# Per-row variance of a 64 MB tensor: how 88 of 128 columns are summed and squared, and by which engine

## The chip, the core and the metric

The kernel runs on one core of one Trainium2 chip. The core has engines with their own instruction queues that meet only through semaphores: VectorE (DVE), ScalarE (ACT), GpSimd (POOL) and SyncE (SP), which here only starts transfers. TensorE isn't used. Data comes from the chip's main memory (HBM) into an on-chip memory of 128 partitions (SBUF) over 16 DMA engines. PSUM is a second, smaller on-chip memory that ACT and DVE can write.

The metric is the time of the program on the device in microseconds (us). The kernel before takes 165.54 us, the median of 3 runs (165.43 to 165.58).

## The reference

```python
x: (32, 512, 1024) float32
mean_sq = np.mean(x**2, axis=-1)
sq_mean = np.mean(x, axis=-1)**2
return (mean_sq - sq_mean).astype(np.float32)
```

So each of 16384 rows of 1024 numbers is reduced to one number, its variance. 67.1 MB are read and 64 KB are written, and every number read is used once.

## The kernel before

**Tiling.** The 16384 rows are spread over 128 partitions, 128 rows to each. A "column" is one row of each partition: 128 x 1024 numbers, 0.52 MB. Column numbers run from 0 to 127. In memory the first 16 columns form one block and the other 112 a second one (`BLOCKS`), so that inside a block the columns of one partition lie next to each other. `load` (L40) brings n neighbouring columns in one transfer from SP's queue: n x 4 KB in a row for each partition.

**Body.** Columns 0 to 103 come in 13 loads of 8 columns (L143 to L151), into three rotating tiles `xt`. A load into a tile waits until DVE and ACT are through with what the tile held before. Of each 8 columns, ACT takes 3 or 2 (in turn) and DVE the other 5 or 6.

- An ACT column (`act_cols`, L117) takes two instructions over 1024 numbers. A Copy (L121) whose accumulator gives minus the mean, and then a Square (L129) which takes that mean as its bias operand and whose accumulator gives the variance, written straight into the result tile `mv`. The elementwise results go to scrap tiles: the Copies of a group to `junk[0]`, `junk[1]`, `junk[2]`, all Squares to `junk[3]`. Reading the accumulator is an instruction of its own in the profile (ACTIVATION_READ_ACCUMULATOR).
- A DVE column takes two bn_stats (BATCH_NORM_STATS2, L111), one for each half of 512 numbers. Each gives counts, means and sums of squared deviations.
- For the body's DVE columns POOL joins these statistics into variances (`join`, L81 to L108), ten small instructions for many columns at once.

**End.** The last 24 columns have a tile of their own, `xt_end`, and come in loads of 6, 6, 4, 3, 2 and 1 columns (`END_LOADS`), which `END_WHO` deals out to ACT (A) and DVE (D). The statistics of the first two of these loads are joined by POOL. After those, DVE joins each column's two halves itself with a bn_aggr (BATCH_NORM_AGGREGATE, L169). The last two columns come in halves, each half a transfer, so that DVE can begin on the first half (L173 to L179).

**Stores.** Columns 0 to 15 are stored from ACT's queue, the others from SP's queue when all is done (L52).

**What sets the order.** Each engine's queue is in order. The instructions are put into the queues by a planner that follows the order of the program and may move an instruction forward where it expects its engine to be idle; it also adds the semaphore waits. The store from ACT, last in the program, stands in ACT's queue at 140.9 us, before ACT's work on `xt_end`. SP's loads too wait now and then for an earlier transfer, on account of a limited number of transfers in flight.

Of the kernel before, what the change touches and what calls it, by code (L numbers as in the profile page):

```python
# [10 lines left out]
@with_exitstack  # L11
def kernel(
    ctx: ExitStack,
    tc: tile.TileContext,
    x: bass.AP,
    out: bass.AP,
):

    nc = tc.nc
    P = nc.NUM_PARTITIONS
    FP32 = mybir.dt.float32
    ACTF = mybir.ActivationFunctionType
    ALU = mybir.AluOpType

    xf = x.flatten_outer_dims()
    N, D = xf.shape
    assert N % P == 0
    ncols = N // P  # L30
    H = D // 2


    SMALL = 16
    BLOCKS = [(0, SMALL, 0), (SMALL, ncols - SMALL, SMALL * P)]

    def block_of(c):
        return next(b for b in BLOCKS if b[0] <= c < b[0] + b[1])

    def load(dst, c0, n, f0=0, f=D):  # L40

        b0, pitch, row0 = block_of(c0)
        assert c0 + n <= b0 + pitch
        ap = [[pitch * D, P], [D, n], [1, f]] if n > 1 else [[pitch * D, P], [1, f]]
        nc.sync.dma_start(  # L45
            out=dst,
            in_=dataclasses.replace(xf, offset=(row0 + c0 - b0) * D + f0, ap=ap),
        )

    def store(engine, block):  # L50
        b0, pitch, row0 = block
        engine.dma_start(  # L52
            out=dataclasses.replace(out, offset=row0, ap=[[pitch, P], [1, pitch]]),
            in_=mv[:, 1, b0 : b0 + pitch],
        )

    GROUP = 8
    NGROUPS = 13
    END0 = GROUP * NGROUPS
    ACT_OF_GROUP = (3, 2)  # L60

    END_LOADS = [6, 6, 4, 3, 2, 1]
    END_WHO = "AADDDDAADDDDDADDDADADA"
    BATCH = (2, 6, 2)

    xpool = ctx.enter_context(tc.tile_pool(name="xpool", bufs=3))
    spool = ctx.enter_context(tc.tile_pool(name="spool", bufs=4))
    opool = ctx.enter_context(tc.tile_pool(name="opool", bufs=1))

    mv = opool.tile([P, 2, ncols], FP32)  # L70
    neg_mean = opool.tile([P, ncols], FP32)
    junk = [opool.tile([P, D], mybir.dt.bfloat16, name=f"junk{i}") for i in range(4)]
    xt_end = opool.tile([P, ncols - END0, D], FP32)
    stats_of = {}

    def stats_block(name, groups, each):

        st = opool.tile([P, groups * each, 2, 6], FP32, name=name)
        return st

    def join(st, groups, each, first, step, skip):  # L81

        n = groups * each
        part = st.rearrange("p n h (e s) -> p n (h e) s", s=3)
        mean, m2 = part[:, :, :, 1], part[:, :, :, 2]
        two = opool.tile([P, n, 2], FP32, name=f"two{first}")
        mu = opool.tile([P, n, 1], FP32, name=f"mu{first}")
        dev = opool.tile([P, n, 4], FP32, name=f"dev{first}")
        g = nc.gpsimd
        g.tensor_tensor(out=two, in0=mean[:, :, 0:2], in1=mean[:, :, 2:4], op=ALU.add)  # L90
        g.tensor_tensor(out=mu, in0=two[:, :, 0:1], in1=two[:, :, 1:2], op=ALU.add)
        g.tensor_scalar(out=mu, in0=mu, scalar1=0.25, scalar2=None, op0=ALU.mult)  # L92
        g.tensor_tensor(out=dev, in0=mean, in1=mu.to_broadcast([P, n, 4]), op=ALU.subtract)  # L93
        g.tensor_tensor(out=dev, in0=dev, in1=dev, op=ALU.mult)  # L94
        g.tensor_scalar(out=dev, in0=dev, scalar1=D / 4.0, scalar2=None, op0=ALU.mult)  # L95
        g.tensor_tensor(out=dev, in0=dev, in1=m2, op=ALU.add)  # L96
        g.tensor_tensor(out=two, in0=dev[:, :, 0:2], in1=dev[:, :, 2:4], op=ALU.add)  # L97
        g.tensor_tensor(out=mu, in0=two[:, :, 0:1], in1=two[:, :, 1:2], op=ALU.add)
        var = mv[:, 1, first : first + groups * step].rearrange(
            "p (g k) -> p g k", k=step  # L100
        )[:, :, skip : skip + each]
        g.tensor_scalar(  # L102
            out=var,
            in0=mu.rearrange("p (g k) o -> p g (k o)", k=each),
            scalar1=1.0 / D,
            scalar2=None,
            op0=ALU.mult,
        )  # L108

    def dve_half(stats, h, xh):  # L110
        nc.vector.bn_stats(out=stats[:, h, :], in_=xh)  # L111

    def dve_halves(stats, xcol):
        dve_half(stats, 0, xcol[:, :H])
        dve_half(stats, 1, xcol[:, H:])

    def act_cols(cols):  # L117

        s = D ** -0.5
        for i, (xcol, c) in enumerate(cols):  # L120
            nc.scalar.activation(  # L121
                out=junk[i],
                in_=xcol,
                func=ACTF.Copy,
                scale=-s / D,
                accum_out=neg_mean[:, c : c + 1],
            )
        for i, (xcol, c) in enumerate(cols):
            nc.scalar.activation(  # L129
                out=junk[3],  # L130
                in_=xcol,
                func=ACTF.Square,
                scale=s,
                bias=neg_mean[:, c : c + 1],
                accum_out=mv[:, 1, c : c + 1],
            )

    body = []
    for par in range(2):
        groups = len(range(par, NGROUPS, 2))  # L140
        each = GROUP - ACT_OF_GROUP[par]
        body.append((stats_block(f"stats{par}", groups, each), groups, each))
    for g in range(NGROUPS):  # L143
        c0 = g * GROUP
        xt = xpool.tile([P, GROUP, D], FP32, name="xt")
        load(xt, c0, GROUP)
        skip = ACT_OF_GROUP[g % 2]
        act_cols([(xt[:, k, :], c0 + k) for k in range(skip)])
        st, _, each = body[g % 2]
        for k in range(skip, GROUP):  # L150
            dve_halves(st[:, g // 2 * each + k - skip, :, :], xt[:, k, :])  # L151
    for par, (st, groups, each) in enumerate(body):
        join(st, groups, each, par * GROUP, 2 * GROUP, ACT_OF_GROUP[par])

    nb, step, skip = BATCH
    each = step - skip
    st_end = stats_block("stats_end", nb, each)
    k = 0
    for b, n in enumerate(END_LOADS):
        load(xt_end[:, k : k + n, :] if n > 1 else xt_end[:, k, :], END0 + k, n)  # L160
        mine = range(k, k + n)
        act_cols([(xt_end[:, j, :], END0 + j) for j in mine if END_WHO[j] == "A"])
        for j in mine:
            if END_WHO[j] == "D" and b < nb:
                dve_halves(st_end[:, b * each + j - k - skip, :, :], xt_end[:, j, :])
            elif END_WHO[j] == "D":
                stats = spool.tile([P, 2, 6], FP32, name="stats")
                dve_halves(stats, xt_end[:, j, :])
                nc.vector.bn_aggr(out=mv[:, :, END0 + j], in_=stats)  # L169
        if b == nb - 1:  # L170
            join(st_end, nb, each, END0, step, skip)
        k += n
    for j in range(k, ncols - END0):  # L173
        stats = spool.tile([P, 2, 6], FP32, name="stats")
        for h in range(2):
            xh = xt_end[:, j, h * H : (h + 1) * H]
            load(xh, END0 + j, 1, h * H, H)
            dve_half(stats, h, xh)
        nc.vector.bn_aggr(out=mv[:, :, END0 + j], in_=stats)  # L179

    store(nc.scalar, BLOCKS[0])
    store(nc.sync, BLOCKS[1])
# [30 lines left out]
```

## Time and profile before

| | us |
|---|---|
| median of 3 runs | 165.54 |
| span of the profiled execution, first to last instruction | 163.5 |
| DVE, ACT, POOL busy in it | 106.1, 94.9, 10.2 |
| first load of 8 columns in, engines start | 12.74 |
| last aggregate of DVE ends | 160.84 |
| final store issued | 160.98 |

The profile shows one execution. The run's time is some 2 us longer than its span, since it includes what lies before the first and after the last instruction; the profiled execution has no separate time beside its span. In the lists, a line of the timeline gives the start, the duration and the instruction, with its output and inputs, and in brackets how long the engine was idle before and what ended that. Instructions of one engine may overlap a little at their ends, so what one more of them costs is the distance from start to start, which is shorter than the duration. "128x512" is 128 partitions by 512 numbers.

### The profile page before, as it was taken

What the parts mean: (1) busy time and instruction counts of PE and PEld (TensorE: products, weight loads), DVE (VectorE), ACT (ScalarE), POOL (GpSimd) and SP (SyncE); (2) the same over time, 40 slices, a digit from 0 to 9 for tenths busy, and PEclk for the clock granted to TensorE, in tenths of its full rate; (3) what the DMA queues carried; (4) which work ended last, traced back from release to release, by engine and by line L of the source; (5) the groups of instructions that cost most, each with busy time, mean ns of one, the idle gap of its engine ahead of it and who ended that gap; (6) DMA issues with size and microseconds to landing.
All of it is one profiled execution on the core that took longest, in us unless ns stands there. A gap on an engine that the chain in (4) does not pass through costs nothing.

```text
span 163.5 us, 462 instructions
## 1 busy us (share of the span) xinstructions
DVE 106.1 (65%) x182; ACT 94.9 (58%) x165; POOL 10.2 (6%) x34
## 2 busy tenths in 40 slices
DVE  0008559393793917949097682949559396859993
ACT  3008756195733937349390693809755195499892
POOL 0000000000000000000000000000000635302200
DMA  7899898998999999999999999999999999999970
GB/s 257 385 481 417 385 513 385 417 481 385 481 417 385 485 409 393 497 393 425 465 393 473 417 393 505 393 401 489 393 465 425 421 391 475 391 440 409 408 291 14
DMA packets 3602, 67.19 MB, mean 411 GB/s; under 512 B 656, under 2 KB 656, under 8 KB 1296
## 3 DMA queue, kind: packets, MB, share of 16 engines
q1 hardware_dynamic: 3456, 67.17, 96.3%
q10 hardware_dynamic: 144, 0.01, 0.1%
q14 instruction: 2, 0.02, 0.0%
HBM read 67.11 MB, written 0.07 MB: 411 GB/s over the span
## 4 chain that ended last, share of the span: by engine, by line
DMA 79%; DVE 11%; ACT 8%; issue 0%; SPq 0%
DMA xt<-in_x_dram 62%; DMA xt_end<-in_x_dram 17%; DVE stats L111 10%; ACT junk L129 4%; ACT junk L121 4%; DVE mv L179 0%; SPq L45 0%
## 5 line engine op out<-in xcount | busy, mean ns | idle before, releaser
L111 DVE BATCH_NORM_STATS2 stats<-xt 128x6 f32<-128x512 f32 x142 | 85.5, 678 | 50.7 <-DMA xt<-in_x_dram 50.7
L121 ACT ACTIVATE junk<-xt 128x1024 bf16<-128x1024 f32 x33 | 34.5, 1046 | 59.2 <-DMA xt<-in_x_dram 59.2
L129 ACT ACTIVATE junk<-xt,neg_mean 128x1024 bf16<-128x1024 f32 x33 | 37.7, 1142 | 0.6
L111 DVE BATCH_NORM_STATS2 stats_end<-xt_end 128x6 f32<-128x512 f32 x16 | 9.7, 680 | 3.7 <-DMA xt_end<-in_x_dram 3.7
L121 ACT ACTIVATE junk<-xt_end 128x1024 bf16<-128x1024 f32 x8 | 8.4, 1046 | 5.0 <-POOL mv L102 4.2
L111 DVE BATCH_NORM_STATS2 stats<-xt_end 128x6 f32<-128x512 f32 x16 | 10.1, 666 | 0.1
L129 ACT ACTIVATE junk<-xt_end,neg_mean 128x1024 bf16<-128x1024 f32 x8 | 9.2, 1144 | 0.2
L90 POOL TENSOR_TENSOR two<-stats 128x72 f32<-128x72 f32 (+1 forms) x2 | 0.8, 406 | 131.3 <-DVE stats L111 131.3
L129 ACT ACTIVATION_READ_ACCUMULATOR junk<-xt,neg_mean 128x1 f32 x33 | 6.2, 186 | 0.0
L121 ACT ACTIVATION_READ_ACCUMULATOR junk<-xt 128x1 f32 x33 | 6.2, 186 | 0.0
L121 ACT ACT_TABLE_LOAD x1 | 1.3, 1283 | 0.7 <-PEq L197 0.7
L121 ACT ACTIVATION_READ_ACCUMULATOR junk<-xt_end 128x1 f32 x8 | 1.5, 186 | 0.0
L129 ACT ACTIVATION_READ_ACCUMULATOR junk<-xt_end,neg_mean 128x1 f32 x8 | 1.5, 186 | 0.0
L95 POOL TENSOR_SCALAR dev<-dev 128x144 f32<-128x144 f32 (+2 forms) x3 | 1.4, 472 | 0.3
L169 DVE BATCH_NORM_AGGREGATE mv<-stats 128x2 f32<-128x12 f32 x6 | 1.2, 203 | 0.1
L94 POOL TENSOR_TENSOR dev<-dev 128x144 f32<-128x144 f32 (+2 forms) x3 | 1.1, 362 | 0.2
L96 POOL TENSOR_TENSOR dev<-dev,stats 128x144 f32<-128x144 f32 (+1 forms) x2 | 1.1, 528 | 0.2
L93 POOL TENSOR_TENSOR dev<-stats,mu 128x144 f32<-128x144 f32 (+1 forms) x2 | 0.9, 470 | 0.2
L102 POOL TENSOR_SCALAR mv<-mu 128x36 f32<-128x36 f32 (+2 forms) x3 | 0.9, 287 | 0.3
L92 POOL TENSOR_SCALAR mu<-mu 128x36 f32<-128x36 f32 (+2 forms) x3 | 0.9, 284 | 0.3
L97 POOL TENSOR_TENSOR two<-dev 128x72 f32<-128x72 f32 (+2 forms) x3 | 0.8, 276 | 0.2
L90 POOL TENSOR_TENSOR two<-stats_end 128x16 f32<-128x16 f32 x1 | 0.2, 233 | 8.9 <-DVE stats_end L111 8.9
(9 smaller groups left out, 2.7 us busy)
## 6 DMA issues: line engine op xcount, KB each, us to landing
xt<-in_x_dram SPq DMA_DIRECT2D x13, 4096.0 KB, 22.2
xt_end<-in_x_dram SPq DMA_DIRECT2D x2, 3072.0 KB, 32.2
xt_end<-in_x_dram SPq DMA_DIRECT2D x1, 2048.0 KB, 40.0
xt_end<-in_x_dram SPq DMA_DIRECT2D x1, 1536.0 KB, 43.2
xt_end<-in_x_dram SPq DMA_DIRECT2D x1, 1024.0 KB, 45.1
xt_end<-in_x_dram SPq DMA_DIRECT2D x4, 256.0 KB, 15.3
xt_end<-in_x_dram SPq DMA_DIRECT2D x1, 512.0 KB, 36.7
out_dram<-mv SPq DMA_DIRECT2D x1, 56.0 KB, 1.6
```

Of the source, the lines that this page charges most:

```text
L90: g.tensor_tensor(out=two, in0=mean[:, :, 0:2], in1=mean[:, :, 2:4], op=ALU.add)
L92: g.tensor_scalar(out=mu, in0=mu, scalar1=0.25, scalar2=None, op0=ALU.mult)
L93: g.tensor_tensor(out=dev, in0=mean, in1=mu.to_broadcast([P, n, 4]), op=ALU.subtract)
L94: g.tensor_tensor(out=dev, in0=dev, in1=dev, op=ALU.mult)
L95: g.tensor_scalar(out=dev, in0=dev, scalar1=D / 4.0, scalar2=None, op0=ALU.mult)
L96: g.tensor_tensor(out=dev, in0=dev, in1=m2, op=ALU.add)
L97: g.tensor_tensor(out=two, in0=dev[:, :, 0:2], in1=dev[:, :, 2:4], op=ALU.add)
L102: g.tensor_scalar(out=var, in0=mu.rearrange("p (g k) o -> p g (k o)", k=each), scalar1=1.0 / D, scalar2=None, op0=ALU.mult,)
L111: nc.vector.bn_stats(out=stats[:, h, :], in_=xh)
L121: nc.scalar.activation(out=junk[i], in_=xcol, func=ACTF.Copy, scale=-s / D, accum_out=neg_mean[:, c : c + 1],)
L129: nc.scalar.activation(out=junk[3], in_=xcol, func=ACTF.Square, scale=s, bias=neg_mean[:, c : c + 1], accum_out=mv[:, 1, c : c + 1],)
L169: nc.vector.bn_aggr(out=mv[:, :, END0 + j], in_=stats)
```

## The change

The work is dealt out anew, in three batches, by a letter for each column.

- S (97 columns): DVE only sums the column. One `tensor_reduce` does it for all S columns of a load, so for 16 x 1024 numbers per partition in the first four loads. ACT squares the column and gets the mean of the squares from its accumulator.
- A (10 columns): ACT squares the column, and also gets the sum by a Copy.
- J (12 columns): two bn_stats, joined by POOL.
- D (8 columns): two bn_stats and a bn_aggr on DVE.

For S and A columns POOL computes mean square minus squared mean (`moments`) for a whole batch: a product, a scaling, and one subtraction for each load of the batch that has such columns (7, 4 and 4). ACT's scrap output is four rotating tiles in PSUM in float32, 8 KB less SBUF than the bf16 ones before; its Square has no bias operand any more. The loads are 16 columns four times, then 8 three times, then 8, 8, 6, 5, then 4, 3, 3, 2; the 5 columns 110 to 114 straddle two tiles and are two transfers. All data goes into three rotating tiles of 16 columns. The last column comes in pieces of 512, 256, 128 and 128 numbers, with a bn_stats each and one bn_aggr.

```diff
-    GROUP = 8
-    NGROUPS = 13
-    ACT_OF_GROUP = (3, 2)
-    END_LOADS = [6, 6, 4, 3, 2, 1]
-    END_WHO = "AADDDDAADDDDDADDDADADA"
+    BATCHES = [
+        ["S" * 16] * 4 + ["S" * 8] * 3,
+        ["SSSAAJJJ", "SSSAAJJJ", "SSAJJJ", "SAJJJ"],
+        ["ADDD", "ADD", "ADD", "AD"],
+    ]
+    LAST = [512, 256, 128, 128]
+    SLOT = 16
...
-    junk = [opool.tile([P, D], mybir.dt.bfloat16, name=f"junk{i}") for i in range(4)]
-    xt_end = opool.tile([P, ncols - END0, D], FP32)
+    ppool = ctx.enter_context(tc.tile_pool(name="ppool", bufs=1, space=bass.MemoryType.PSUM))
+    junk = [ppool.tile([P, D], FP32, name=f"junk{i}") for i in range(4)]
+    def act(xcol, func, scale, accum):
+        nonlocal njunk
+        nc.scalar.activation(
+            out=junk[njunk % len(junk)], in_=xcol, func=func, scale=scale, accum_out=accum
+        )
+        njunk += 1
+
+    def moments(b, total, meansq, runs):
+        g = nc.gpsimd
+        n = total.shape[1]
+        sq = opool.tile([P, n], FP32, name=f"sq{b}")
+        g.tensor_tensor(out=sq, in0=total, in1=total, op=ALU.mult)
+        g.tensor_scalar(out=sq, in0=sq, scalar1=1.0 / (D * D), scalar2=None, op0=ALU.mult)
+        at = 0
+        for c0, m in runs:
+            g.tensor_tensor(
+                out=mv[:, 1, c0 : c0 + m],
+                in0=meansq[:, at : at + m],
+                in1=sq[:, at : at + m],
+                op=ALU.subtract,
+            )
+            at += m
...
+    def stats_of(st, xcol):
+        for h in range(2):
+            nc.vector.bn_stats(out=st[:, h, :], in_=xcol[:, h * H : (h + 1) * H])
+
+    def slot(c):
+        i = c // SLOT
+        if i not in tiles:
+            tiles[i] = xpool.tile([P, SLOT, D], FP32, name="xt")
+        return tiles[i], c % SLOT
...
+        for who in loads:
...
+            if ns:
+                xt, k = slot(c)
+                nc.vector.tensor_reduce(
+                    out=total[:, im : im + ns],
+                    in_=xt[:, k : k + ns, :],
+                    axis=AXIS.X,
+                    op=ALU.add,
+                )
...
+            for j, w in enumerate(who):
+                if w in "SA":
+                    act(cols[j], ACTF.Square, D**-0.5, meansq[:, im : im + 1])
+                    if w == "A":
+                        act(cols[j], ACTF.Copy, 1.0, total[:, im : im + 1])
+                    im += 1
+                elif w == "J":
+                    stats_of(st[:, ij, :, :], cols[j])
+                    ij += 1
+                else:
+                    st1 = opool.tile([P, 2, 6], FP32, name=f"one{c + j}")
+                    stats_of(st1, cols[j])
+                    nc.vector.bn_aggr(out=mv[:, :, c + j], in_=st1)
+            c += n
+        if nm:
+            moments(b, total, meansq, mruns)
+        if nj:
+            join(b, st, jruns)
...
+    for h, f in enumerate(LAST):
+        load(xt[:, k, f0 : f0 + f], c, 1, f0, f)
+        nc.vector.bn_stats(out=st1[:, h, :], in_=xt[:, k, f0 : f0 + f])
+        f0 += f
+    nc.vector.bn_aggr(out=mv[:, :, c], in_=st1)
```

`join` keeps its nine steps before the last and now ends with one scaling for each load of its batch (4).

## The prediction

> **What bounds the kernel now.** I read the page first: busy shares, slices, chain, loads.
>
> ```profile
> DVE 106.1 (65%) x182; ACT 94.9 (58%) x165; POOL 10.2 (6%) x34
> DMA  7899898998999999999999999999999999999970
> DMA 79%; DVE 11%; ACT 8%; issue 0%; SPq 0%
> xt<-in_x_dram SPq DMA_DIRECT2D x13, 4096.0 KB, 22.2
> ```
>
> No engine is full; the transfers are, from slice 2 to slice 38. So the kernel is the load stream plus what follows its end. The stretches by window agree (columns: length, DVE, ACT, POOL busy, clock, DMA share, GB/s):
>
> ```profile
> 22.40:120.40 98.00, 66.24 (x110) 57.01 (x100) 0.00 (x0) 1.00 1.01 433
> 157.00:158.00 1.00, 0.92 (x3) 0.97 (x2) 0.00 (x0) 1.00 1.05 385
> 159.00:160.00 1.00, 0.97 (x4) 0.97 (x3) 0.00 (x0) 1.00 0.02 6
> ```
>
> Then the timeline, for landing times, prices and the tail (start, length, instruction):
>
> ```profile
> 12.74 1.06 ACT L121 ACTIVATE junk<-xt 128x1024 bf16<-128x1024 f32 x1 [10.74 <-DMA xt<-in_x_dram]
> 13.80 1.04 ACT L121 ACTIVATE junk<-xt 128x1024 bf16<-128x1024 f32 x1
> 14.75 0.18 ACT L121 ACTIVATION_READ_ACCUMULATOR junk<-xt 128x1 f32 x1
> 17.13 1.15 ACT L129 ACTIVATE junk<-xt,neg_mean 128x1024 bf16<-128x1024 f32 x1
> 18.41 1.15 ACT L129 ACTIVATE junk<-xt,neg_mean 128x1024 bf16<-128x1024 f32 x1
> ...
> 130.18 1.06 ACT L121 ACTIVATE junk<-xt 128x1024 bf16<-128x1024 f32 x1 [5.12 <-DMA xt<-in_x_dram]
> ...
> 150.03 0.20 POOL L91 TENSOR_TENSOR mu<-two 128x8 f32<-128x8 f32 x1
> 150.32 0.24 POOL L92 TENSOR_SCALAR mu<-mu 128x8 f32<-128x8 f32 x1
> 150.64 0.25 POOL L93 TENSOR_TENSOR dev<-stats_end,mu 128x32 f32<-128x32 f32 x1
> ...
> 151.60 1.24 DVE L111 BATCH_NORM_STATS2 stats<-xt_end 128x6 f32<-128x512 f32 x2
> 152.75 0.20 DVE L169 BATCH_NORM_AGGREGATE mv<-stats 128x2 f32<-128x12 f32 x1
> 152.86 0.64 DVE L111 BATCH_NORM_STATS2 stats<-xt_end 128x6 f32<-128x512 f32 x1
> ...
> 160.63 0.21 DVE L179 BATCH_NORM_AGGREGATE mv<-stats 128x2 f32<-128x12 f32 x1
> 160.98 0.35 SPq L52 DMA_DIRECT2D out_dram<-mv  x1
> ```
>
> What to see. Column 8 is in at 12.74, column 104 at 130.18: 1.2233 us a column, so n columns are in at 12.74 + 1.2233(n - 8); n = 125 gives 155.87, and ACT did stop waiting for that load at 155.86. A Copy takes 1.04 start to start; two end 2.19 after their load (14.93 - 12.74). Squares stand 1.28 apart because all write junk 3. Two bn_stats halves and an aggregate take 1.26 (151.60 to 152.86), a half 0.60. Small POOL steps that follow from each other take 0.29 and 0.32. The final store issues 0.14 after the last aggregate (160.84).
>
> The sum goes against this execution, span 163.5; the median of the runs is 165.54, 2.04 more, which I carry over unchanged.
>
> **The load stream.** 20 loads instead of 23, the same bytes. SP's three issues fewer (0.33 to 0.43 each) lie beside a busy queue: nothing. In the body a load waits for the slot three earlier: the fourth 16 columns need slot 0, free at about 39.6, while the queue holds work until 61.7. Three slots cover it; were a slot held until the queue ran dry, each late microsecond would be lost. SP's waits on earlier transfers (12.1 us once, on the small store from ACT) stay: the last loads then issued at 149.9 and 150.3, and landed in time. Whether rows of 64 KB move at another rate than rows of 32 KB no row shows. Ends: 455 GB/s, the best stretch of ten (92 to 102), or 385, the stretch with the shortest rows. I take the same rate, since share 1.01 leaves no gap between transfers to remove.
>
> **The first loads.** DVE and ACT begin at 22.53 (n = 16) instead of 12.74. 9.8 us of free engine time are given away, and the question is whether each catches up before the tail.
>
> **ACT.** Removed: 41 Copies and 41 biased Squares. Added: 107 Squares (97 S, 10 A) and 10 Copies. A Square without a bias tile, into four rotating outputs in PSUM, has no row, and no row writes PSUM: lower end 0.95 (Copy less its accumulator's 0.09), upper 1.28 (Squares as they stand). I take the Copy's 1.04, because the reasons for 1.28 (one shared output, an operand from a tile) are both taken away. Sixteen cost 16.6 against 19.6 of landing. Slot 3 lands at 81.2: done 97.9; the three loads of 8 at 106.2, 114.5, 122.8; the next 7 instructions at 130.1, when n = 104 lands (130.2). Caught up; the excess is hidden. The store that ACT issues waits for POOL's first result, two or three microseconds about 124, which the later loads absorb (7.3 of work per 9.8).
>
> The Trainium skill, ScalarE: Activation LUTs, under "What ACT_TABLE_LOAD costs", gives 186 ns + 0.833 N for immediate scale and bias and some 93 ns more for a pointer operand: 1.04 and 1.13 at N = 1024, and the durations here, 1040 and 1147, agree within 15 ns. Were the zero bias still a pointer, two Squares at the end would by that be late by about 0.1.
>
> **DVE.** Removed: 174 half-column bn_stats and 8 aggregates. Added: sums over 97 columns (11 instructions), 24 halves for J, 16 halves and 8 aggregates for D, four pieces and one aggregate for the last column. A sum over 16 x 1024 has no row; the nearest is bn_stats. Upper end: 0.60 for 512 as it stands, 1.204 a column. Lower: less 0.11, the start-to-start share of an aggregate (152.75 to 152.86), 0.98 a column. I take 0.07 as the fixed part (0.678 long, 0.60 apart): 1.06 a column, 17.0 per slot. Slot 3 is then done at 98.2, the loads of 8 at 106.7, 115.2, 123.7, then 6.8 each to 130.5 and 137.3; n = 110 lands at 137.5. Caught up, with little to spare.
>
> The Trainium skill, VectorE: DVE Perf Modes, "Rules for kernel authors", speaks against the part: expect 1x from tensor_reduce, the slowest DVE operation. At that page's 0.96 GHz a slot would be 17.07 us, still under 19.6; by it the sum is the same. No run here shows it yet.
>
> **POOL ahead of the tail.** Removed: three joins of 10 steps. Added: 9 steps for columns 0 to 87, 6 and 13 for columns 88 to 114. The last of these start when DVE has its last J (148.1): 13 x 0.33 = 4.3, done at 152.4, eight microseconds before POOL is wanted again. Nothing, unless DVE is late.
>
> **The tail, on the path.** Columns 125 and 126 come in one load, in at 12.74 + 119 x 1.2233 = 158.31. ACT then does Square and Copy of column 125: 2.19, so 160.50. Now POOL is on the path, which it wasn't: the last A columns get their variance from it. The wake-up is 0.08 (149.63 to 149.71). Product 0.29, scaling 0.32, then four subtractions of one column each. They don't depend on each other, and no row shows such a run: upper end 0.29 apart as dependent steps (sum 1.68), lower the 0.03 between the constants' memsets at the start (sum 0.90). I take 0.20, their own length: 0.29 + 0.32 + 3 x 0.20 + 0.20 = 1.41. POOL ends at 160.50 + 0.08 + 1.41 = 161.99, and the store goes at 162.13.
>
> DVE beside it: two D columns from 155.89 to 158.41, column 126 to 159.67, then 0.60 + 0.33 + 0.20 + 0.27 for the pieces (slope as above) and 0.21 for the aggregate: 161.3. The pieces have landed by then: the first half-column of before came at 157.81 where the rate says 157.70, so four pieces at 0.11 extra each are in at 160.0, before DVE reads the last at 160.8. The cut of the last column is worth nothing: DVE still arrives through column 126.
>
> **Sum.** Store at 162.13 instead of 160.98: +1.15. Forecast 165.54 + 1.15 = 166.7. Its own range: POOL's ends -0.5 and +0.3 (DVE's 161.3 holds from below at +0.5), ACT's -0.2 and +0.2: 166.0 to 167.2.
>
> **Rivals.**
> Faster: longer rows speed up the loads. Place: the first 64 columns, 78.3 us. It decides once they run 1.9% faster (1.5 us); at 455 instead of 433 GB/s it's 3.8 us less, 162.9; half that 164.8. For it: stretches of 441 and 455. Against: share 1.01, and 32 KB and 24 KB rows both at 1.22 us a column.
> DVE falls behind: from slot 3 to the end of column 124 there are 49 r + 14.4 (J) + 8.8 (seven D) in 77.2, so it decides from r = 1.10 a column. At 1.204 the end moves by 5.1 past 161.3: store 166.5, total 171.1. For it: the thin margin. Against: a fixed part of nothing in bn_stats isn't credible.
> ACT falls behind: from about 1.18 a column; at 1.28 it goes without a break from 22.5, 117 x 1.28 = 149.8, to 172.3, some 177.4 in all. For it: the Squares of now. Against: their shared output is gone.
> No change: POOL's steps overlap, sum 0.9, and the loads gain 0.3 to 0.7: 165.6 to 166.0.
>
> **Chances.** Forecast 0.58; DVE behind 0.12; ACT behind 0.05; either behind by less, 167.2 to 168.5, 0.04; no change 0.07; loads faster 0.14. Faster or slower means by over 0.2% (0.33 us), about what can be told from no change: faster 0.14, same 0.07, slower 0.79. The range 165.0 to 169.5 leaves out most of the faster case and the worse half of the engines behind.
>
> **What would show it.** Right: DMA share near 1 until 158; the sum of 16 columns near 17 us; Squares 1.04 apart; ACT and DVE waiting for loads again after 137; POOL last before the store, its subtractions after 160.5. Wrong: DVE or ACT without idle time from 81 to the end; the load of column 126 in at 157 or sooner; POOL done before DVE.

## The result, and the profile after

The changed kernel takes 166.38 us (median of 4 runs, 166.18 to 166.54) against 165.56 us before: 1.0049 times as long, with a 95% interval of 1.0035 to 1.0064. It's slower by 0.82 us; the forecast was 1.15 us slower, 166.7. A second comparison of the same two kernels, made later, gave 1.0055 (1.0041 to 1.0069).

The page's view of busy shares, transfers and chain after the change:

```profile
DVE 130.9 (80%) x64; ACT 123.8 (75%) x235; POOL 7.5 (5%) x38
...
DMA  7989996996998899699699998999989999999950
...
DMA 58%; DVE 37%; ACT 1%; POOL 1%; issue 0%; POOLq 0%; ACTq 0%; SPq 0%
...
xt<-in_x_dram SPq DMA_DIRECT2D x5, 4096.0 KB, 31.3
```

DVE and ACT are much busier, yet the transfers go on to slice 38 as before. Four slices of the first half show only 6 tenths, but over longer stretches little is missing: the share is 0.97 from 20 to 60 us (1.00 before) and 1.00 from 60 to 100, and the first 64 columns are in by 80.79, no later than before (81.61). The 37% that the chain gives to DVE is not a loss by itself: a chain that is followed backwards passes through sums that had no waiting between them, while the loads ran beside them. SP's wait for the small store from ACT's queue, now 17.6 us instead of 12.1, isn't one either: the share is 1.00 from 130 to 156, and the load of columns 125 and 126 comes on time. POOL, which wasn't in the chain before, is in it now with 1%. The end of the timeline shows why (start, length, instruction):

```profile
158.37 1.03 ACT L73 ACTIVATE junk<-xt 128x1024 f32<-128x1024 f32 x1 [0.31 <-DMA xt<-in_x_dram]
...
159.42 1.01 ACT L73 ACTIVATE junk<-xt 128x1024 f32<-128x1024 f32 x1
159.67 0.68 DVE L196 BATCH_NORM_STATS2 stlast<-xt 128x6 f32<-128x512 f32 x1
160.26 0.20 DVE L183 BATCH_NORM_AGGREGATE mv<-one 128x2 f32<-128x12 f32 x1
160.37 0.76 DVE L196 BATCH_NORM_STATS2 stlast<-xt 128x6 f32<-128x256 f32 x3
160.37 0.18 ACT L73 ACTIVATION_READ_ACCUMULATOR junk<-xt 128x1 f32 x1
160.64 0.20 POOL L83 TENSOR_TENSOR sq<-total 128x4 f32<-128x4 f32 x1 [7.92 <-ACT junk L73]
160.93 0.23 POOL L84 TENSOR_SCALAR sq<-sq 128x4 f32<-128x4 f32 x1
161.16 0.27 DVE L198 BATCH_NORM_AGGREGATE mv<-stlast 128x2 f32<-128x24 f32 x1
161.24 0.62 POOL L87 TENSOR_TENSOR mv<-meansq,sq 128x1 f32<-128x1 f32 x4
161.88 0.35 SPq L58 DMA_DIRECT2D out_dram<-mv  x1
```

Columns 125 and 126 are there at 158.3, where the rate of the kernel before has them too. ACT needs until 160.55 for column 125, POOL until 161.86, and only then does the store go, at 161.88 instead of 160.98. DVE is through at 161.43, so it lies 0.4 under POOL.

What the engines waited for (total, times, longest), and DVE's timeline in the middle:

```profile
...
ACT junk L73 <- DMA xt<-in_x_dram: 33.0, 8, 20.7
...
DVE total L161 <- DMA xt<-in_x_dram: 29.1, 4, 22.7
ACT junk L73 <- POOL mv L87: 3.0, 1, 3.0
DVE one L127 <- DMA xt<-in_x_dram: 1.2, 2, 0.7
```

```profile
61.45 17.22 DVE L161 TENSOR_REDUCE total<-xt 128x16 f32<-128x16384 f32 x1 [2.23 <-DMA xt<-in_x_dram]
80.79 46.26 DVE L161 TENSOR_REDUCE total<-xt 128x16 f32<-128x16384 f32 x5 [2.13 <-DMA xt<-in_x_dram]
...
148.43 1.88 DVE L127 BATCH_NORM_STATS2 one<-xt 128x6 f32<-128x512 f32 x3 [0.52 <-DMA xt<-in_x_dram]
...
155.81 1.88 DVE L127 BATCH_NORM_STATS2 one<-xt 128x6 f32<-128x512 f32 x3 [0.69 <-DMA xt<-in_x_dram]
```

A sum of 16 columns takes 17.2. From 80.79 on DVE has no pause until the one of 0.52 before 148.43: it did catch up with the loads, but only just.

This profiled execution is the quickest of the four; its span is 164.4, and its time is 166.18, 1.78 more than the span. The median span is 164.6. For the kernel before, the median span beside the later runs is 163.5 and the part outside it 2.0 (1.95 to 2.00 in three sets). So the span grew by 1.1 us, and 0.2 came back outside it.

### The profile page after: what moved, and what is told of

Read it like the earlier page. It is cut to its first block, busy times and chain, and to the rows that moved or that the text cites. A ratio compares the mean times of both kernels' runs of the same rounds, so it can differ in the third digit from the quotient of the medians.

```text
span 164.4 us, 426 instructions
## 1 busy us (share of the span) xinstructions
DVE 130.9 (80%) x64; ACT 123.8 (75%) x235; POOL 7.5 (5%) x38
## 4 chain that ended last, share of the span: by engine, by line
DMA 58%; DVE 37%; ACT 1%; POOL 1%; issue 0%; POOLq 0%; ACTq 0%; SPq 0%
DMA xt<-in_x_dram 51%; DVE total L161 37%; DMA out_dram<-mv 8%; ACT junk L73 1%; POOL sq L84 0%; POOL mv L87 0%; POOL sq L83 0%; POOLq L227 0%; ACTq L227 0%; SPq L51 0%; ACTq L73 0%; POOLq L87 0%
## 5 line engine op out<-in xcount | busy, mean ns | idle before, releaser
L73 ACT ACTIVATE junk<-xt 128x1024 f32<-128x1024 f32 x117 | 117.8, 1007 | 36.0 <-DMA xt<-in_x_dram 33.0
L161 DVE TENSOR_REDUCE total<-xt 128x16 f32<-128x16384 f32 (+4 forms) x11 | 104.7, 9551 | 29.1 <-DMA xt<-in_x_dram 29.1
L73 ACT ACTIVATION_READ_ACCUMULATOR junk<-xt 128x1 f32 x117 | 21.9, 187 | 0.0
L127 DVE BATCH_NORM_STATS2 st<-xt 128x6 f32<-128x512 f32 x24 | 14.6, 677 | 0.0
L127 DVE BATCH_NORM_STATS2 one<-xt 128x6 f32<-128x512 f32 x16 | 10.0, 664 | 1.2 <-DMA xt<-in_x_dram 1.2
L87 POOL TENSOR_TENSOR mv<-meansq,sq 128x16 f32<-128x16 f32 (+5 forms) x15 | 2.5, 206 | 0.2
L183 DVE BATCH_NORM_AGGREGATE mv<-one 128x2 f32<-128x12 f32 x8 | 1.6, 199 | 0.1
L196 DVE BATCH_NORM_STATS2 stlast<-xt 128x6 f32<-128x128 f32 (+2 forms) x4 | 1.4, 402 | 0.0
L84 POOL TENSOR_SCALAR sq<-sq 128x88 f32<-128x88 f32 (+2 forms) x3 | 0.9, 316 | 0.3
L115 POOL TENSOR_SCALAR mv<-mu 128x3 f32<-128x3 f32 x4 | 0.8, 232 | 0.1
```

What stands on the lines that cost most here:

```text
L73: nc.scalar.activation(out=junk[njunk % len(junk)], in_=xcol, func=func, scale=scale, accum_out=accum)
L84: g.tensor_scalar(out=sq, in0=sq, scalar1=1.0 / (D * D), scalar2=None, op0=ALU.mult)
L87: g.tensor_tensor(out=mv[:, 1, c0 : c0 + m], in0=meansq[:, at : at + m], in1=sq[:, at : at + m], op=ALU.subtract,)
L115: g.tensor_scalar(out=mv[:, 1, c0 : c0 + m], in0=mu[:, at : at + m, 0], scalar1=1.0 / D, scalar2=None, op0=ALU.mult,)
L127: nc.vector.bn_stats(out=st[:, h, :], in_=xcol[:, h * H : (h + 1) * H])
L161: nc.vector.tensor_reduce(out=total[:, im : im + ns], in_=xt[:, k : k + ns, :], axis=AXIS.X, op=ALU.add,)
```

## The experiments

Theory: the whole loss lies after the last whole load, and its cause is that POOL's six steps for the last A columns now stand between ACT and the store. DVE's end, 0.4 under it, comes next. Rivals: the new loads and the late start of the engines cost time in the body; or the loads set the end whatever is done.

**POOL taken out of the end** (`t_direct`). The last batch's A columns become B columns: ACT makes the variance itself.

```diff
-        ["ADDD", "ADD", "ADD", "AD"],
+        ["BDDD", "BDD", "BDD", "BD"],
...
+                elif w == "B":
+                    nm1 = opool.tile([P, 1], FP32, name=f"nm{c + j}")
+                    act(cols[j], ACTF.Copy, -(D**-0.5) / D, nm1)
+                    nc.scalar.activation(
+                        out=junk[njunk % len(junk)], in_=cols[j], func=ACTF.Square,
+                        scale=D**-0.5, bias=nm1, accum_out=mv[:, 1, c + j : c + j + 1],
+                    )
```

> The changed kernel, but the four A columns of the last batch (115, 119, 122, 125) get their variance from ACT alone, by a Copy and a Square with the mean as bias, so POOL has nothing after the join of columns 88 to 114. Theory (POOL's last six steps are what the store waits for, and DVE's end at 161.43 lies just under them): the store issues at 161.45 instead of 161.88, the time is about 0.4 us less than the changed kernel's, 166.0. Rival (the new load stream or the body is what costs): the store stays at 161.9 and the time at 166.4.

Measured: 165.97 us, 0.4 less than the changed kernel; 1.0030 times the kernel before (1.0018 to 1.0041). The timeline's end:

```profile
158.60 1.03 ACT L73 ACTIVATE junk<-xt 128x1024 f32<-128x1024 f32 x1 [0.23 <-DMA xt<-in_x_dram]
...
160.84 0.19 ACT L180 ACTIVATION_READ_ACCUMULATOR junk<-xt,nm 128x1 f32 x1
161.30 0.27 DVE L206 BATCH_NORM_AGGREGATE mv<-stlast 128x2 f32<-128x24 f32 x1
161.71 0.35 SPq L58 DMA_DIRECT2D out_dram<-mv  x1
```

The time is as expected. The loads of this execution came 0.2 later than in the first profile, so the store at 161.71 belongs beside the 162.11 of the changed kernel's second profile below, where ACT starts on column 125 at the same 158.60: 0.4 sooner. DVE now ends last, at 161.57, and the store follows 0.14 later, where it followed POOL by 0.02. So of the 1.1 us by which the span grew, POOL's steps account for 0.4. The rest stays, because DVE, which has column 126 and the last column to do, ended only 0.4 before POOL.

**POOL made longer** (`t_pool_long`).

```diff
+        for _ in range(4 if b == 2 else 0):
+            g.tensor_scalar(out=sq, in0=sq, scalar1=1.0, scalar2=None, op0=ALU.mult)
```

> The changed kernel with four more POOL steps in the last batch (the scaled squares are multiplied by 1.0 four times). Theory: every one of them, 0.31 us from start to start, is on the path: store at 161.88 + 1.25 = 163.1, time 167.6. Rival (DVE, ACT or the loads set the end): POOL has time to spare and the time stays at 166.4.

Measured: 167.65 us, 1.27 more than the changed kernel (1.23 more than its second measurement); 1.0132 (1.0119 to 1.0146). Four steps of 0.31 make 1.24, so each is on the path:

```profile
161.32 0.27 DVE L200 BATCH_NORM_AGGREGATE mv<-stlast 128x2 f32<-128x24 f32 x1
161.48 1.14 POOL L86 TENSOR_SCALAR sq<-sq 128x4 f32<-128x4 f32 x4
162.70 0.61 POOL L89 TENSOR_TENSOR mv<-meansq,sq 128x1 f32<-128x1 f32 x4
163.34 0.35 SPq L58 DMA_DIRECT2D out_dram<-mv  x1
```

**The end of the kernel before on the new body** (`t_old_end`).

```diff
-        ["ADDD", "ADD", "ADD", "AD"],
+        ["D", "BDDD", "BDD", "BD", "B"],
-    LAST = [512, 256, 128, 128]
+    LASTS = [[512, 512], [512, 512]]
```

> The changed kernel up to column 114, and from there the end of the kernel before: loads of 1, 4, 3, 2, 1 columns with D and biased ACT columns, and the last two columns in halves. Theory (all of the loss lies after the last whole load): store at 161.0 to 161.1, time 165.5 to 165.7, the same as the kernel before. Rival (starting the engines 9.9 us later, or loads of 16 columns, costs): still 0.4 us or more above the kernel before.

Measured: 165.33 us; 0.9987 times the kernel before (0.9979 to 0.9996).

```profile
157.92 1.38 DVE L205 BATCH_NORM_STATS2 stlast<-xt 128x6 f32<-128x512 f32 x2
...
160.72 0.21 DVE L207 BATCH_NORM_AGGREGATE mv<-stlast 128x2 f32<-128x12 f32 x1
161.07 0.35 SPq L58 DMA_DIRECT2D out_dram<-mv  x1
```

The store is back at 161.07. So columns 0 to 114 in the new form cost nothing, though both engines start ten microseconds later: the loss was all in the end. The 0.2 us below the expectation isn't in the span (median 163.6, against 163.5 before) but outside it (1.78 against 2.00).

**The cut of the last column** (`t_direct_512`), on the version without POOL in the end.

```diff
-    LAST = [512, 256, 128, 128]
+    LAST = [512, 512]
```

> As the run with the direct A columns, and the last column in two halves instead of 512, 256, 128, 128. Theory (DVE reaches the last column late, through column 126, so the small pieces only add instructions): DVE ends 0.1 to 0.2 us sooner, store at 161.3, time 165.8. Rival (the cut of the last column saves waiting for data): later than with four pieces, by 0.2 to 0.4 us.

Measured: 166.00 us, 1.0030 (1.0020 to 1.0041), the same as with four pieces; 165.8 was expected. From the last whole column's bn_stats to the end DVE took 2.74 (158.73 to 161.47) against 2.92 (158.65 to 161.57) with four pieces: 0.18 sooner, as the theory has it, but the loads of this execution were 0.08 later, and the medians don't show the rest. What is shown is that the small pieces gain nothing.

**Shorter first loads** (`b_loads8`).

```diff
-        ["S" * 16] * 4 + ["S" * 8] * 3,
+        ["S" * 8] * 11,
```

> The changed kernel with the first 64 columns in eight loads of 8 columns instead of four of 16, each with its own sum of 8 columns (two loads share a slot). Theory (the stream moves at one rate whatever the length of a row, and a start at 12.8 instead of 22.7 is hidden, since both engines catch up before the end anyway): store within 0.2 us of 161.9, time 166.2 to 166.6, last load of whole columns in at 158.3 as before; both engines wait for loads more often. Rival (rows of 64 KB are faster, or the late start costs): the time moves by over 0.3 us, up in the first case, down in the second.

Measured: 166.75 us, 1.0073 (1.0059 to 1.0087), above the 166.2 to 166.6 expected, beside 166.53 for the next run on the same chip (`b_sbuf`), which has the long loads. The early start gains nothing, so that half of the rival falls. In the profiled execution, the quickest of five at 166.50, the store goes at 162.16, beside 162.11 in the changed kernel's second profile below. The other half, that rows of 64 KB are faster, stays open: the eight loads may cost 0.2 to 0.4 us, but the intervals overlap. Both engines waited for nearly every load, as said (DVE's sums 14 times, ACT 16; DVE's row of the waits, and then two lines of the timeline):

```profile
DVE total L161 <- DMA xt<-in_x_dram: 28.3, 14, 12.9
```

```profile
81.10 8.69 DVE L161 TENSOR_REDUCE total<-xt 128x8 f32<-128x8192 f32 x1 [1.03 <-DMA xt<-in_x_dram]
...
162.16 0.35 SPq L58 DMA_DIRECT2D out_dram<-mv  x1
```

**ACT's scrap output in SBUF** (`b_sbuf`).

```diff
-    junk = [ppool.tile([P, D], FP32, name=f"junk{i}") for i in range(4)]
+    junk = [opool.tile([P, D], mybir.dt.bfloat16, name=f"junk{i}") for i in range(4)]
```

> The changed kernel with ACT's scrap output in SBUF in bf16, as in the kernel before, instead of PSUM in float32. Theory (what counts on ACT is the distance from start to start, 1.04 us in both kernels): Squares last 1.04 instead of 1.01 but stay 1.04 apart, time 166.2 to 166.6. Rival (writing PSUM is what lets ACT keep up): Squares 1.08 or more apart, ACT doesn't wait for loads after 137, and the last Copy ends later by 0.1 us or more.

Measured: 166.53 us, 1.0058 (1.0046 to 1.0071), no difference. Two Squares in a row here, and two of the changed kernel:

```profile
23.88 1.04 ACT L73 ACTIVATE junk<-xt 128x1024 bf16<-128x1024 f32 x1
...
24.92 1.04 ACT L73 ACTIVATE junk<-xt 128x1024 bf16<-128x1024 f32 x1
```

```profile
24.78 1.00 ACT L73 ACTIVATE junk<-xt 128x1024 f32<-128x1024 f32 x1
...
25.82 1.00 ACT L73 ACTIVATE junk<-xt 128x1024 f32<-128x1024 f32 x1
```

Into PSUM they last 1.00 instead of 1.04, but the next one starts 1.04 later in both.

**More work for DVE** (`b_dve_more`).

```diff
-        ["SSSAAJJJ", "SSSAAJJJ", "SSAJJJ", "SAJJJ"],
+        ["SSSAJJJJ", "SSSAJJJJ", "SSAJJJ", "SAJJJ"],
```

> The changed kernel with one column of each of the loads 88 to 95 and 96 to 103 moved from ACT (A) to DVE (J): 2.4 us more for DVE and 4.2 less for ACT. Theory (DVE has just caught up with the loads in the changed kernel: it waits for them only 0.52 and 0.69 us in all after 81 us): the extra 2.4 us use up 1.2 of waiting and push the rest past the end, DVE ends at about 162.6 instead of 161.43, after POOL, and the time is 167.0 to 167.3. Rival (DVE has more room than that): DVE's end moves by less than 0.3 us, time 166.4.

Measured: 166.76 us, 1.0075 (1.0063 to 1.0088).

```profile
161.40 0.61 POOL L87 TENSOR_TENSOR mv<-meansq,sq 128x1 f32<-128x1 f32 x4
162.11 0.27 DVE L198 BATCH_NORM_AGGREGATE mv<-stlast 128x2 f32<-128x24 f32 x1
162.44 0.35 SPq L58 DMA_DIRECT2D out_dram<-mv  x1
```

DVE has taken POOL's place at the end, at 162.38 (expected 162.6), and the time is 0.3 above the changed kernel's second measurement, 166.42. The mechanism holds. The time expected, 167.0 to 167.3, was a quarter of a microsecond too high, mostly because DVE ended 0.2 sooner than expected.

**One sum for each column** (`b_reduce1`).

```diff
-                nc.vector.tensor_reduce(
-                    out=total[:, im : im + ns],
-                    in_=xt[:, k : k + ns, :],
+                for j in range(ns):
+                    nc.vector.tensor_reduce(
+                        out=total[:, im + j : im + j + 1],
+                        in_=xt[:, k + j, :],
```

> The changed kernel with one sum instruction for each S column instead of one for each load: 97 instead of 11 on DVE, the same numbers read. Theory (DVE is at its limit after 81 us; one sum of 1024 stands 1.12 us from the next instruction, against 1.08 per column inside a long one): 49 columns after 81 us cost 2.0 us more, of which 1.2 are waiting that DVE had, so DVE ends at about 162.2 and the store goes at 162.4, 0.5 us later than in the changed kernel, time 166.9. Rival (the length of the instruction doesn't matter): 166.4. Beside it, the part of the time that lies outside the span, 2.0 us in the kernel before and 1.8 in the changed one: if it goes with the number of DVE instructions (182, 64, and some 150 here), it's back near 2.0 here; if not, 1.8.

Measured: 167.21 us, 1.0105 (1.0089 to 1.0120), 0.8 above the changed kernel on the same chip.

```profile
81.22 9.11 DVE L162 TENSOR_REDUCE total<-xt 128x1 f32<-128x1024 f32 x8 [1.56 <-DMA xt<-in_x_dram]
...
160.72 0.20 POOL L83 TENSOR_TENSOR sq<-total 128x4 f32<-128x4 f32 x1 [5.42 <-ACT junk L73]
...
162.57 0.27 DVE L199 BATCH_NORM_AGGREGATE mv<-stlast 128x2 f32<-128x24 f32 x1
162.90 0.35 SPq L58 DMA_DIRECT2D out_dram<-mv  x1
```

Single sums of 1.21 stand (9.11 - 1.21)/7 = 1.13 apart, against 1.07 a column in the long one. From the start of the fourth 16 columns to the start of the last J columns DVE took 65.9 (81.22 to 147.11) instead of 63.5 (80.93 to 144.40 in `again`), 2.4 more, where 2.0 was expected; the 1.2 of waiting that DVE had takes half of that. DVE ends at 162.84, 1.25 later than in `again`, and the time is 0.3 above the 166.9 expected. So the backlog from 81 us on reaches the end, and putting a load's columns into one instruction is what keeps DVE under POOL. Outside the span lie 1.76, so the 0.2 us there doesn't go with the number of DVE instructions.

**The changed kernel once more** (`again`).

> The changed kernel itself, unchanged, beside the run with single sums, so that the two are compared on one chip: 166.2 to 166.6 by every theory, 1.8 us of it outside the span, store at 161.8 to 162.2.

Measured: 166.42 us, 1.0055 (1.0041 to 1.0069), span 164.6, which is also the median span. The last whole load's columns start ACT at 158.60, and the store issues at 162.11.

```profile
158.60 1.03 ACT L73 ACTIVATE junk<-xt 128x1024 f32<-128x1024 f32 x1 [0.38 <-DMA xt<-in_x_dram]
...
160.87 0.20 POOL L83 TENSOR_TENSOR sq<-total 128x4 f32<-128x4 f32 x1 [8.02 <-ACT junk L73]
...
162.11 0.35 SPq L58 DMA_DIRECT2D out_dram<-mv  x1
```

**A version meant to beat both** (`t_best`). DVE takes column 125 and ACT column 126, so DVE comes to the last column without delay.

```diff
-        ["ADDD", "ADD", "ADD", "AD"],
+        ["D", "BDDD", "BDD", "BD", "D", "B"],
-    LAST = [512, 256, 128, 128]
+    LASTS = [[512, 256, 256]]
```

> The body of the changed kernel up to column 114; then loads of 1, 4, 3, 2, 1, 1 columns with D columns and ACT columns with a biased Square (no POOL at the end), DVE takes column 125, ACT takes column 126, and the last column comes in 512, 256, 256. Theory (the end is set by whichever engine gets the last whole column on top of its share): ACT ends column 126 at 160.7 to 160.8, DVE the last column at 160.6, store at 160.8 to 160.9, time 165.0 to 165.3, 0.2 to 0.5 us under the kernel before. Rival (the landing of the last pieces sets the end whatever is done): 165.5, as the kernel before.

Measured: 165.36 us, 0.9990 (0.9981 to 0.9999).

```profile
158.94 1.03 ACT L73 ACTIVATE junk<-xt 128x1024 f32<-128x1024 f32 x1 [0.32 <-DMA xt<-in_x_dram]
...
160.91 0.24 DVE L207 BATCH_NORM_AGGREGATE mv<-stlast 128x2 f32<-128x18 f32 x1
161.17 0.19 ACT L180 ACTIVATION_READ_ACCUMULATOR junk<-xt,nm 128x1 f32 x1
161.42 0.35 SPq L58 DMA_DIRECT2D out_dram<-mv  x1
```

The profiled execution is the slowest of the eleven, 165.66, with a span of 163.9. In it DVE ends 0.4 sooner than with a D column 126, but column 126 in a load of its own starts ACT at 158.94 instead of 158.4 to 158.6, and ACT ends at 161.36, not at 160.7 to 160.8. This span is 0.3 above the median one, so part of the lateness is this execution's own. The expectation, 165.0 to 165.3, was missed: the median span is 163.6, against 163.5 for the kernel before. So neither this nor `t_old_end` gains anything in the span on the kernel before; the 0.2 us by which they win lie outside it.

## Why the prediction was right

**The body.** Said: the rate of the loads stays, and both engines catch up. Shown: the last whole load comes at 158.37 in the profile and 158.60 in the second one (said 158.31), and with the old end the new body costs nothing. DVE caught up when it was said to. It was to be through with the columns up to 103 at 137.3, just before the next load, and it came to that load at 137.38 (137.66 in `b_loads8`, where DVE had to wait for it). That agreement holds some luck: the 40 columns from the fourth slot on took 43.0 (80.79 to 123.80) where the prediction's 1.06 a column makes 42.5, and the start was 0.4 sooner than the 81.2 said. The price was 1.07 in a long sum and 1.12 in a sum of one. After that DVE had almost no room: it paused twice, for 0.52 and 0.69, and the two runs with more work for DVE show how little that was. ACT was put at 130.1 and was free of work at 147.5; the 3.0 us of waiting for POOL at 122, which the prediction had foreseen at two to three, lie between.

**The sum and the Square.** 17.0 was taken for a sum of 16 columns between 15.7 and 19.3: it took 17.22. The page of the Trainium skill that spoke against the sum, VectorE: DVE Perf Modes, "Rules for kernel authors", expects one element per cycle; by its clock that is an estimate of 17.07, and this case's 17.22 agrees within 1%. The Square was taken at the Copy's 1.04 between 0.95 and 1.28, and was 1.04 apart. The timeline of the kernel before gives each of the two reasons for the old 1.28 a part: with its operand from a tile, a Square takes 1.15 when a Copy into another output follows (157.04 to 158.19), and 1.28 when a Square into the same output follows.

**POOL in the end.** This was the step that set the store, and both runs on it agree: taken out, the time fell by 0.4 down to DVE's end, made longer by 1.24 it rose by 1.27. That DVE lay close under it was also said (161.3 against 161.99). Its terms, said and measured in the profile:

| step | said | measured |
|---|---|---|
| ACT's two instructions end | 160.50 | 160.55 |
| wake-up of POOL | 0.08 | 0.09 |
| product, scaling | 0.61 | 0.60 |
| four subtractions | 0.80 | 0.62 |
| POOL's end to the store | 0.14 | 0.02 |
| store | 162.13 | 161.88 |

Two terms were too large. The subtractions, which don't depend on each other, were put 0.20 apart between the bounds 0.03 and 0.29, and stand 0.14 apart ((0.62 - 0.19)/3). The step from the last result to the store was read from one after DVE; after POOL it's 0.02, while in `t_direct` it's 0.14 again after DVE (but 0.06 after DVE in `b_dve_more` and `b_reduce1`).

**The total.** In the execution with the median span the store goes 1.13 later than in the profile of before, against 1.15 said. That is luck: there the last load was 0.23 later than in the first profile, which made up for the two terms. The time then grew by only 0.82 because of the sentence "2.04 more, which I carry over unchanged": outside the span it's 1.76 to 1.82 with the changed kernel and all its variants (medians), and 1.95 to 2.00 with the kernel before beside them. That is the term that was mis-sized in the sum; it isn't explained. It doesn't go with the number of DVE instructions (64 and about 150 gave 1.79 and 1.76), with PSUM (1.82 without) or with the number of loads (1.77 with four more).

**DVE's end and the cut.** Said 161.3 with the cut worth nothing: measured 161.43, and two halves were no slower than four pieces in `t_direct_512`.

**The rivals.** Loads faster: the fourth 16 columns did start DVE sooner, at 80.79 against 81.61 before, but nothing of that was left at column 126. Engines behind: not in this kernel, but one column more in each of two loads, or single sums, were enough for DVE; at 1.13 a column it was past the 1.10 that the rival named as its threshold, and 1.25 late. ACT behind: its Squares kept 1.04. Two totals of the prediction don't follow from its own terms: ACT's end at 172.3 instead of 160.5 would make 178.5 and not 177.4, and no change 165.5 to 165.9 and not 165.6 to 166.0; neither bears on the forecast.

The row of the kernel before for that start (its load of columns 56 to 63, the last of the first 64):

```profile
81.61 1.88 DVE L111 BATCH_NORM_STATS2 stats<-xt 128x6 f32<-128x512 f32 x3 [3.69 <-DMA xt<-in_x_dram]
```

## What to carry to other kernels

When loads fill the whole time and the engines keep up with them, a new division of the work among the engines is worth what it does after the last load; write down that chain, instruction by instruction, with every engine that hands something on. A cheap method for the body (a sum here, a square there, a join elsewhere) can be the wrong one for the last columns, because its join comes after everything: keep the body's method away from the end. And an engine that starts late and is only 3% faster than needed (DVE here, 1.07 a column where 1.10 was allowed) must be followed to the end of the work, since its backlog shrinks by the difference only.

## What the runs showed that was not expected

- Writing ACT's unused result to PSUM shortens the instruction from 1.04 to 1.00 us, and nothing comes of it: with an accumulator read after each, the next one starts 1.04 later from either memory. The Trainium skill, ScalarE: Activation LUTs, in the remark on the placement of the engines under "Step-by-step: what each stage is for", calls PSUM the output of lower latency; the duration agrees, the spacing here doesn't change.
- The store's issue follows a POOL result by 0.02 to 0.03 us in every run. A DVE result it follows by 0.14 in four kernels (the one before, `t_direct`, `t_direct_512`, `t_old_end`) and by 0.06 in two (`b_dve_more`, `b_reduce1`); why is open.
- Four POOL subtractions on 1 column each, which don't need each other, stand 0.14 apart; steps on 4 columns that need each other stand 0.29 to 0.31 apart.
- The part of the time outside the span differs between two kernels of the same launch by 0.2 us, steadily (1.76 to 1.82 against 1.95 to 2.00). A forecast by spans alone misses that; what makes it is open.
